# Gates, u, v and the output projection of an encoder layer by Strassen's form over two token halves

## The chip, the core and the metric

The kernel runs on one core of a Trainium2 chip. The core has TensorE (PE, matrix products into PSUM), VectorE (DVE), ScalarE (ACT), GpSimd (POOL) and SyncE (SP); each works through its own instructions in order and waits on semaphores. DMA transfers are started from the queues of SP, ACT and POOL. The metric is device time in microseconds, as the median of several runs.

## The reference

One layer of a hybrid encoder, 1024 tokens by 1024 features, fp32. What is computed, cut to what matters here:

```python
mod = silu(c) @ w_ada + b_ada                    # six vectors of 1024: sh1, sc1, gt1, sh2, sc2, gt2
h = rmsnorm(x, norm1_g) * (1 + sc1) + sh1
u, v, q, k, va, gate_a, gate_b = split(h @ w_in) # widths 512, 512, 512, 128, 128, 1024, 1024
# branch A: gelu(u) * (W_s mixed over chunks of 128 tokens of rmsnorm(gelu(v)) + b)
a_out = gmlp_branch(u, v, ...) @ w_a
# branch B: attention over |t - s| <= 128, 8 heads of 64, 2 key heads, ALiBi, a sink logit
b_out = window_attention_branch(q, k, va, ...) @ w_b
merged = sigmoid(gate_a) * a_out + sigmoid(gate_b) * b_out
x = x + gt1 * (merged @ w_o)
h2 = rmsnorm(x, norm2_g) * (1 + sc2) + sh2
f_gate, f_up = split(h2 @ w_ffn_in)              # 2816 each
x = x + gt2 * ((silu(f_gate) * f_up) @ w_ffn_out)
```

## The kernel before

**Three products for one.** fp32 precision comes from splitting both operands of a product into a rounded high part and a low part. `mm3` (line 154) issues three matmuls for each tile: high by high, high by low, low by high. A weight block of 128x1024 is made ready by `unit` (line 146): a load on SP's queue into a tile `raw`, a cast on ACT into `wh`, and a subtraction on DVE (or POOL) into `wl`. The pool `wpool` holds three of each. The same is done to activations by `split` (line 310). Nearly all matmuls are 128x128 weights by 512 columns.

**Halves.** The 1024 tokens are worked in two halves of 512 by `half(0)` and `half(1)` (line 513). Each half goes through these steps, all in one function:

- q and k: eight steps over the 1024 features. In half 0 each step also makes its slice of h and takes the dot products of the first modulation vectors (`ada_dot`, line 197; a 128x1024 multiply and sum on DVE).
- v (`v_product`, line 648), among the norms of q and k and their transposes on PE.
- attention in eight steps (the loop at line 789: `scores`, `exps`, `normalise`, `transposed`, `values`). Between these PE is kept full by `fill`, which pops parts of the products for u and for the first four gates (`u_filler`, `gate_filler`). Weight lows there are made on POOL (`prepare`).
- mixing of the gMLP branch over chunks, and its transposes.
- a loop over eight output blocks d of 128 features (line 868): two gates of 24 matmuls, two branch projections of 12, a multiply of each by its gate, their sum, and its split into `mH`, `mL`. `ada_next` loads further modulation weights and takes their dot products on DVE.
- a loop over d for w_o (line 919): 24 matmuls, the residual sum x1, its square for the next norm, a store of x1 to DRAM (`x1d`) on POOL's queue, and the modulation of h for the other half or of h2 for the FFN.

**FFN.** Behind both halves `open_ffn` closes the pools of attention and opens the FFN's. The FFN's two products over 1024 tokens are already in Strassen's form: the matrices are cut in 2x2 blocks (token halves by halves of the features), and seven block products of sums of blocks take the place of eight. Its order is written out by hand under `tc.manual_schedule()` (line 1281).

**What sets the order.** Loads on SP's queue keep the program's order (`load`, line 126), first in, first out. Instructions of PE, DVE, ACT and POOL keep it where `in_order[0]` is true (the recorder `Engine.call`, line 75, through which every operation goes; so most rows of the profile say L75). Elsewhere a scheduler orders them by readiness, and the written program decides among equals. Tiles come from pools with a fixed number of buffers: `mid` has 8 of 128x2048, `hpool` 4, `t2` 4 of 128x512. PSUM has two groups of four banks, `mm` and `at`. A load whose tile is still being read waits, and with it what stands behind it on SP's queue.

Of the kernel before, what the change touches and what calls it, by code (L numbers as in the profile page):

```python
# [38 lines left out]
def kernel(  # L39
# [48 lines left out]
    hpool = ctx.enter_context(pool("hpool", 4))  # L88
    mid = ctx.enter_context(pool("mid", 8))
# [3 lines left out]
    psum = ctx.enter_context(pool("psum", 4, space=PSUM))  # L93

# [23 lines left out]
    def hid():  # L118
        return hpool.tile([P, 2048], F32R, tag="h", name=nm("h")).rearrange(
            "p (a b) -> p a b", a=4  # L120
        )
# [9 lines left out]

    def after(ins, prev):
# [8 lines left out]
    def raw_unit(src):  # L141
        r = wpool.tile([P, UNIT], F32, tag="raw", name=nm("raw"))
        load(r, src)
        return r
# [80 lines left out]

    apool_ctx = ExitStack()
# [3 lines left out]
    silu_c = apool.tile([P, D], F32, tag="silu_c", name="silu_c")  # L230
# [236 lines left out]
    EARLY = 6  # L467
    firsts, raw2 = {}, []
    ffn_ctx = ExitStack()
    fps = []  # L470

    def open_ffn():

        apool_ctx.close()
        fp = ffn_ctx.enter_context(pool("ffn"))
        fps.append(fp)
        for part in range(2):
            t = fp.tile([P, 2048], F32R, tag=f"b22{'hl'[part]}", name=nm("first"))
            firsts[part] = t
# [15 lines left out]
    sums = []  # L495
    ada_queue = (
# [12 lines left out]

    def x_rows(hf, k):  # L510
        return xT[k * P : (k + 1) * P, hf * HALF : (hf + 1) * HALF]

    def half(hf):
# [62 lines left out]
        for k in range(KT):  # L576
# [23 lines left out]
            elif k == 0:  # L600
                wq, wk = early.pop(0), early.pop(0)
# [24 lines left out]
        if hf == 0:  # L626
            attention_constants()
        else:
            col_rstd(sums[0], NT, rcol[2])
# [5 lines left out]
        wvs = [unit(w_v[0], V)]  # L635
# [12 lines left out]
        def v_product(k):  # L648
            wv = wvs[k // 2]
            o = (k % 2) * 512  # L650
            for t in range(NT):
                cols = slice(t * P, (t + 1) * P)
                mm3(vps[t], (hH[k // 4][:, k % 4, cols], hL[k // 4][:, k % 4, cols]),
                     (wv[0][:, o : o + 512], wv[1][:, o : o + 512]), k == 0, k == KT - 1)

        srcs = [w_u[k] for k in range(4)] + [w_gb[0], w_ga[0], w_gb[1], w_ga[1], w_s]
        srcs += [w_ab[0], w_ab[1]]
        units = []
        ups = []
        gates0 = []  # L660

        due = [0]

        def prepare(eng=G):
            if srcs:
                units.append(unit(srcs.pop(0), eng))
# [855 lines left out]
```

## Time and profile before

| | |
|---|---|
| median of 3 runs | 1257.25 us (1256.49 to 1257.72) |
| profiled execution, span | 1255.1 us |
| PE, PE weight load | 1234.1 us, 1025.1 us |
| DVE, ACT, POOL | 861.5 us, 543.5 us, 132.7 us |
| DMA | 214.25 MB, mean 171 GB/s |
| chain that ended last | PE 86%, DVE 6%, ACT 3%, DMA 3% |

The profiled execution is one run under the hardware profiler; its span is the time from its first to its last recorded event, 2.15 us below the median of the timed runs. A group row names the line, the engine, the operation, output and inputs by the program's names, the shape and the count; then the total busy time and the mean of one in ns; then the idle time of the engine in front of them and what ended it. A busy engine can be a stretched one: matmuls overlap, so that the mean of a PE row (390 ns) is longer than the step from one matmul to the next.

### The profile page before, as it was taken

Reading aid. Unit: us, or ns where it says so; the run is one execution under the profiler, and the core shown is the slowest. Engines: PE = TensorE matmul, PEld = TensorE weight load, DVE = VectorE, ACT = ScalarE, POOL = GpSimd, SP = SyncE. Lnnn points to the kernel's source line nnn. Section 1 sums busy time; section 2 is a strip of 40 time slices with the busy share of each in tenths; the row PEclk is TensorE's granted clock in tenths of the full one; section 3 lists DMA queues with packets and bytes.
Section 4 is the critical chain, followed back from the end, with each engine's and each line's share of the span. In section 5 each row is a group of like instructions: output and inputs, shape, how many; then the busy total and the mean of one; then the engine's idle time right before and its main releaser. Section 6 shows DMA issues by size and latency. Waiting matters only on the chain.

```text
span 1255.1 us, 15405 instructions
## 1 busy us (share of the span) xinstructions
PE 1234.1 (98%) x5714; PEld 1025.1 (82%) x5714; DVE 861.5 (69%) x1404; ACT 543.5 (43%) x867; POOL 132.7 (11%) x148
## 2 busy tenths in 40 slices
PE   5999999999999999999999999999999999999998
PEld 4888888888888888888888888888888887888887
DVE  8998875557468786666698766666666666455646
ACT  5467853334257772334454333333333334433342
POOL 0123310000032330000100000001010000010001
PEclk9999999999999999999999999999999999999999
DMA  9422145546522126665712454464554449896652
GB/s 362 169 84 67 52 143 184 177 159 211 197 70 67 51 89 196 201 194 209 250 36 102 147 189 151 154 213 182 205 189 180 168 168 357 280 328 187 196 161 101
DMA packets 67773, 214.25 MB, mean 171 GB/s; under 512 B 7793, under 2 KB 7793, under 8 KB 62450
## 3 DMA queue, kind: packets, MB, share of 16 engines
q1 hardware_dynamic: 56450, 155.59, 37.5%
q0 software_dynamic: 11248, 57.68, 12.7%
q8 instruction: 45, 0.74, 0.2%
q14 instruction: 30, 0.25, 0.1%
HBM read 170.24 MB, written 42.99 MB: 170 GB/s over the span
## 4 chain that ended last, share of the span: by engine, by line
PE 86%; DVE 6%; ACT 3%; DMA 3%; issue 1%; SPq 0%; POOL 0%; ACTq 0%; DVEq 0%
PE mm L75 47%; PE at L75 39%; DVE mid L75 2%; DVE wl L75 2%; ACT wh L75 1%; DMA mid<-in_w_ada_dram 1%; DMA hs<-in_xT_dram 1%; ACT lb L75 1%; DVE xs L75 0%; DMA mid<-in_xT_dram 0%; ACT mid L75 0%; DVE ws L75 0%; DMA raw<-in_w_o_dram 0%; DVE hid L75 0%; DMA raw<-in_w_q_dram 0%
## 5 line engine op out<-in xcount | busy, mean ns | idle before, releaser
L75 DVE TENSOR_TENSOR wl<-raw,wh 128x1024 fp32r<-128x1024 f32 x147 | 180.7, 1231 | 122.9 <-ACT wh L75 121.5
L75 ACT CAST wh<-raw 128x1024 fp32r<-128x1024 f32 x161 | 168.9, 1053 | 218.7 <-PE mm L75 126.7
L75 PE MATMUL mm<-mid,wh 128*128 128x512 f32 x736 | 227.8, 390 | 0.8 <-DVE mid L75 0.6
L75 PE MATMUL mm<-h,wh 128*128 128x512 f32 x608 | 187.9, 390 | 0.0
L75 PEld LDWEIGHTS mm<-mid,wh 128*128 128x128 f32 x736 | 137.7, 188 | 30.3 <-DVE mid L75 1.0
L75 PE MATMUL mm<-mid,wl 128*128 128x512 f32 x368 | 143.2, 389 | 0.0
L75 PEld LDWEIGHTS mm<-h,wh 128*128 128x128 f32 x608 | 113.7, 188 | 23.4
L75 PE MATMUL mm<-wh,h 128*128 128x512 f32 x384 | 129.7, 399 | 2.4 <-ACT h L75 2.3
L75 PE MATMUL mm<-h,wl 128*128 128x512 f32 x304 | 118.3, 389 | 0.0
L75 DVE TENSOR_TENSOR wl<-ws,wh 128x1024 fp32r<-128x1024 f32 (+1 forms) x55 | 62.0, 1128 | 43.6 <-ACT wh L75 43.6
L75 PEld LDWEIGHTS mm<-wh,h 128*128 128x128 f32 x384 | 71.7, 189 | 17.3 <-ACT h L75 3.2
L75 PEld LDWEIGHTS mm<-mid,wl 128*128 128x128 f32 x368 | 69.1, 188 | 14.4
L75 ACT CAST wh<-ws 128x1024 fp32r<-128x1024 f32 (+1 forms) x55 | 53.6, 974 | 58.6 <-DVE ws L75 42.1
L75 PE MATMUL mm<-wl,h 128*128 128x512 f32 x192 | 75.9, 395 | 0.0
L75 PE MATMUL at<-h,wh 128*128 128x512 f32 x240 | 74.1, 390 | 0.0
L75 PEld LDWEIGHTS mm<-h,wl 128*128 128x128 f32 x304 | 57.1, 188 | 12.0
L75 DVE SCALAR_TENSOR_TENSOR raw<-raw,silu_c 128x1024 f32<-128x1024 f32 x32 | 39.1, 1222 | 34.4 <-DMA raw<-in_w_ada_dram 33.5
L75 DVE TENSOR_TENSOR ol<-raw,oh 128x1024 fp32r<-128x1024 f32 x30 | 36.7, 1224 | 31.6 <-ACT oh L75 29.8
L75 ACT ACTIVATE xs<-xs 128x512 f32<-128x512 f32 x21 | 13.3, 633 | 96.4 <-DVE xs L75 96.4
L75 PE MATMUL at<-wl,wh 128*128 128x512 f32 x136 | 53.0, 390 | 0.7 <-DVE wl L75 0.7
L75 PE MATMUL at<-wh 128*128 128x512 f32 x136 | 53.0, 390 | 0.4 <-DVE mid L75 0.4
L75 PE MATMUL at<-wh,wl 128*128 128x512 f32 x136 | 52.9, 389 | 0.0
(244 smaller groups left out, 2459.8 us busy)
## 6 DMA issues: line engine op xcount, KB each, us to landing
raw<-in_w_ada_dram SPq DMA_DIRECT2D x32, 512.0 KB, 3.5
raw<-in_w_gate_dram SPq DMA_DIRECT2D x28, 512.0 KB, 4.1
tA<-hid POOLq DMA_DIRECT2D x11, 1024.0 KB, 5.0
tB<-hid POOLq DMA_DIRECT2D x11, 1024.0 KB, 4.9
wo<-in_w_out_dram POOLq DMA_DIRECT2D x22, 512.0 KB, 6.3
wS<-wo POOLq DMA_DIRECT2D x11, 1024.0 KB, 5.2
raw<-wS SPq DMA_DIRECT2D x44, 256.0 KB, 3.7
raw<-tB SPq DMA_DIRECT2D x44, 256.0 KB, 4.6
```

Of the source, the lines that this page charges most:

```text
L75: ins = f(*args, **kw)
```

## The change

Strassen's form, which the FFN had, is now used for three more products: both gates together with u and v (they share h), and w_o. The 2x2 blocks of the activations are feature halves by token halves, so that products need sums of h over both token halves; work that stood in each half moves into one stage behind both attentions.

- **Pools.** `hpool` is gone (`hid` takes from `mid`, now 12 buffers); a pool `j` of 6 buffers opens behind the attentions. Ten DRAM arrays hold intermediate results. `astore` stores from ACT's queue (56 transfers).
- **Half 0.** The squares of the other half's x are summed on POOL during q and k (`x_square`), and its modulation runs in attention (`x_mod`), both with their own loads. PE's work among the norms is `bridge_product` (the two feature halves of h times w_u, kept apart); fillers are the products with w_ga. Partial results go to DRAM (`uvd`, `gd`). `u_sums` makes the sums of w_u and w_v blocks on POOL, 128x1024 each, and stores them.
- **Half 1.** `block_sums` reloads the two halves' modulated x (four loads of 1 MB) and makes the blocks T3, T4, n2, t1 during q and k. The bridge takes the sums of w_u and w_v; the fillers take the sums of w_ga and w_gb (`gate_raw_sum`, added on POOL).
- **u and v** are completed by three products of 48 matmuls with DVE sums between (`uv_product`, `uv_out`), and `v_chain` normalises v.
- **Loop over d.** `gate_prep` loads both gate weights and the stored partial gates and makes five sums of 128x512 on POOL; `gate_step` runs three groups of 12 matmuls, each followed by a sum from PSUM on DVE and a tanh. `project` makes four projections of 12 matmuls (two branches, two halves). `merge` adds them and, for d below 6, stores the merged tile on SP's queue. `ada_two` loads 1 MB of modulation weights and takes two dots; there are two of them in each turn up to d = 5.
- **w_o** is laid out in four 512x512 blocks and computed by seven products of 48 matmuls. Block sums of the weights are made on POOL (`wsum`, eight of 128x1024), those of the merged tiles on DVE (`fsum`, `block`). x1, its squares, its stores (on ACT's queue) and the modulation of h2 follow each product.

Matmuls of 512 columns go from 4988 to 4796; those of other sizes are as many as before.

```diff
-    hpool = ctx.enter_context(pool("hpool", 4))
-    mid = ctx.enter_context(pool("mid", 8))
+    mid = ctx.enter_context(pool("mid", 12))
...
+    def ada_two():
+        if not ada_queue:
+            return
+        i = ada_queue[0][0] - GT1
+        r = jt(F32, 2)
+        load(r, w_ada2[i : i + 2].rearrange("a p b -> p a b"))
+        for a in range(2):
+            col, gain = ada_queue.pop(0)
+            ada_dot(r[:, a, :], col)
+            ada_end(col, gain)
...
+    def block_sums(k, hH, hL):
+        if k == 0:
+            for i, (name, src) in enumerate((("a0", x0d), ("a1", x0d), ("b0", x1sd), ("b1", x1sd))):
+                blk[name] = midt(F32, 4)
+                load(blk[name], src[i % 2 * 4 : i % 2 * 4 + 4].rearrange("a p b -> p a b"))
...
+        if k == 1:
+            V.tensor_tensor(flat(b1), flat(b1), flat(b0), op=ALU.subtract)
...
-        def v_product(k):
-            wv = wvs[k // 2]
+        def bridge_product(k):
+            wv = bridge[k // 2]
...
+        def gate_raw_sum(d):
+            r = wpool.tile([P, UNIT], F32, tag="raw", name=nm("raw"))
+            load(r, w_gb[d])
+            x = stream("hs")
+            load(x, w_ga[d][:, :Q])
+            G.tensor_tensor(r[:, :Q], r[:, :Q], x, op=ALU.add)
+            return r
...
+                return [lambda: G.tensor_tensor(a[:, 1], a[:, 0], a[:, 1], op=ALU.add),
+                        lambda: G.tensor_tensor(a[:, 0], a[:, 0], b[:, 0], op=ALU.add),
...
+    jpools.append(ffn_ctx.enter_context(pool("j", 6, reuse_waits="tile")))
...
+    def uv_product(us, t, first):
+        for k in range(4):
+            w, o = us[k // 2], (k % 2) * 512
+            for i in range(NT):
+                cols = slice(i * P, (i + 1) * P)
+                for j, (p, q) in enumerate(((0, 0), (0, 1), (1, 0))):
+                    T.matmul(ubank[i], t[p][:, k, cols], w[q][:, o : o + 512],
+                             start=first and k + j == 0, stop=k == 3 and j == 2,
+                             skip_group_check=True)
...
+    def gate_prep(d):
+        ga, gb = raw_unit(w_ga[d]), raw_unit(w_gb[d])
+        g = gates[d] = jt(F32, 4)
+        load(flat(g), gd[d])
+        G.tensor_tensor(gb[:, Q:], gb[:, :Q], gb[:, Q:], op=ALU.add)
+        G.tensor_tensor(gb[:, :Q], ga[:, :Q], gb[:, Q:], op=ALU.add)
+        G.tensor_tensor(ga[:, Q:], ga[:, Q:], gb[:, :Q], op=ALU.add)
+        for i in (1, 3):
+            G.tensor_tensor(g[:, i, :], g[:, i, :], g[:, 2, :], op=ALU.add)
+        u = unit(None, V, gb)
+        h, l = tmp(F32R), tmp(F32R)
+        split(ga[:, Q:], h, l)
+        gunits[d] = u, (h, l)
+        A.activation(g[:, 0, :], g[:, 0, :], AF.Tanh, scale=0.5)
...
+    for d in range(KT):
+        wab = wabs[d]
+        if d:
+            gate_step(d, 2)
+        gate_step(d + 1, 0)
+        if d:
+            project(d, wab, 1, 0)
+            project(d, wab, 1, 1)
+        else:
+            project(d, wab, 0, 0)
+        gate_step(d + 1, 1)
+        if d + 2 < KT:
+            gate_prep(d + 2)
+        if d:
+            project(d, wab, 0, 0)
+        if d < KT - 1:
+            wabs[d + 1] = unit(w_ab[d + 1])
+        project(d, wab, 0, 1)
...
+        for hf in range(2):
+            merge(d, hf)
+        if d < 6:
+            ada_two()
+            ada_two()
...
+    def wsum(out, a, b):
+        for j in range(2):
+            js = slice(j * UNIT, (j + 1) * UNIT)
+            G.tensor_tensor(flat(out)[:, js], flat(a)[:, js], flat(b)[:, js], op=ALU.add)
...
+    oprod(wu, M11, sA, True)
...
+    block("M21", mf[1, 0])
+    wu = ounits(1)
+    h2m.append(xload(0, 0))
+    wsum(wq4[0], wq4[0], wq4[2])
+    wq4[4] = jt(F32, 4)
+    wsum(wq4[4], wq4[0], wq4[3])
...
+    fsum(t3f, m22, m12, ALU.subtract)
+    fsum(m12, m11, m12, ALU.subtract)
...
+    oprod(wu, blk["M21"], sB, True)
+    block("n2", m11)
+    wu = ounits(4)
...
+    oprod(wu, blk["n2"], sA, False)
+    wsum(wq4[1], wq4[1], wq4[4])
+    wsum(wq4[2], wq4[2], wq4[3])
+    block("T3", t3f)
...
+    oprod(wu, blk["T3"], sA, False)
+    block("T4", m21)
...
+    oprod(wu, blk["T4"], sA, False)
...
+    oprod(wu, blk["t1"], sB, True, range(2))
+    col_rstd(ss, NT, rcol[2])
...
+    oprod(wu, blk["M22"], sB, False)
```

More of the change, by code (lines that the diff above doesn't have):

```diff
@@ L467 @@
     EARLY = 6
+    Q = HALF
     firsts, raw2 = {}, []
[L469 to L479, printed above, removed]
     def first_unit(i):
@@ L495 @@
     sums = []
+    spare = []
+    outs = []
     ada_queue = (
@@ new lines, in ssq, with keep_x1 @@
+    def ssq(x, first, ss, eng=G):
+        if first:
+            A.activation(ss, x, AF.Square)
+        else:
+            q = tmp()
+            A.activation(q, x, AF.Square)
+            eng.tensor_tensor(ss, ss, q, op=ALU.add)
+    def keep_x1(q, hf, d, x):
+        r = (4 * q + d) * P
+        astore(x1d[r : r + P, hf * HALF : (hf + 1) * HALF], x)
+    sA = [at_bank() for _ in range(4)]
+    oprod(wu, M11, sA, True)
+    for i in (2, 3):
+        load_wo(i)
+    load_m(0, 1)
+    block("M21", mf[1, 0])
```

695 lines of the change are left out of this document (492 added, 203 removed).

## The prediction

> **What bounds the kernel now.** I read the page first, for the shares of the engines. The columns are busy time, share of the span, and instructions.
>
> ```profile
> span 1255.1 us, 15405 instructions
> PE 1234.1 (98%) x5714; PEld 1025.1 (82%) x5714; DVE 861.5 (69%) x1404; ACT 543.5 (43%) x867; POOL 132.7 (11%) x148
> PE   5999999999999999999999999999999999999998
> DVE  8998875557468786666698766666666666455646
> POOL 0123310000032330000100000001010000010001
> PEclk9999999999999999999999999999999999999999
> GB/s 362 169 84 67 52 143 184 177 159 211 197 70 67 51 89 196 201 194 209 250 36 102 147 189 151 154 213 182 205 189 180 168 168 357 280 328 187 196 161 101
> ```
>
> PE is busy in every slice but the first, and the clock is never lowered. A busy share of PE can hide half-speed streaming, so the chain that ended last comes next (start, length, what), and then what PE waited for (total, times, longest).
>
> ```profile
> 168.83 109.05 PE mm L75 x481
> 464.33 111.60 PE mm L75 x491
> ```
>
> ```profile
> PE at L75 <- DVE ss L75: 8.4, 1, 8.4
> PE at L75 <- DMA crow<-in_c_dram: 2.4, 1, 2.4
> PE mm L75 <- ACT h L75: 2.3, 2, 1.8
> ```
>
> In the two middle stretches 481 matmuls follow each other in 109.05 us: 0.2267 us each. The waits are nearly all of the start, whose loads and first norm the change leaves alone. The view by stretches of time shows the stages: first half (33 to 328 us), second half (328 to 610), FFN.
>
> ```profile
> 0.00:33.00 33.00, 19.60 (x75) 14.84 (x76) 29.04 (x54) 17.74 (x28) 2.25 (x9) 1.00 0.94 365
> 33.00:80.00 47.00, 46.48 (x259) 39.98 (x258) 42.31 (x95) 22.91 (x50) 12.87 (x11) 1.00 0.35 122
> ...
> 120.00:169.00 49.00, 48.73 (x262) 41.47 (x261) 40.95 (x99) 40.44 (x89) 18.48 (x12) 1.00 0.18 56
> 169.00:285.00 116.00, 116.00 (x521) 96.08 (x520) 68.34 (x102) 38.48 (x51) 2.35 (x2) 1.00 0.54 177
> ...
> 610.00:1250.00 640.00, 638.40 (x2819) 527.08 (x2818) 420.46 (x540) 240.52 (x304) 41.22 (x74) 1.00 0.55 186
> sum 1250.00, PE 1233.13 PEld 1024.61 DVE 860.30 ACT 543.48 POOL 132.72; mean PE 102.76 PEld 85.38 DVE 71.69 ACT 45.29 POOL 11.06
> ```
>
> The columns are window, length, busy time and count of PE, PEld, DVE, ACT, POOL, then granted clock, DMA share, GB/s. PE bounds every stage behind 33 us. DVE is close behind it in the first stage (42.31 of 47) and in attention (40.95 of 49), and has room in the gates (68.34 of 116). So fewer matmuls shorten the run as long as nothing late is put before them, and there is little else to gain: behind 33 us PE is idle 1217 − (1233.13 − 19.60) = 3.5 us.
>
> **The change part by part.** *Matmuls removed.* Gates, u and v were 1152 matmuls of 512 columns in both halves (768 + 192 + 192); seven products for eight leave 1008. For w_o 384 become 336. That is 192 fewer, at 0.2267 us: −43.5 us, all in stages where PE streams without a gap. Ideal span: 1255.1 − 43.5 = 1211.6 us. Everything below is a wait that the new sums and reloads may put before PE. The durations for it:
>
> ```profile
> L75 DVE TENSOR_TENSOR wl<-raw,wh 128x1024 fp32r<-128x1024 f32 x147 | 180.7, 1231 | 122.9 <-ACT wh L75 121.5 <-DMA raw<-tA 1.0
> L75 ACT CAST wh<-raw 128x1024 fp32r<-128x1024 f32 x161 | 168.9, 1053 | 218.7 <-PE mm L75 126.7 <-PE at L75 38.0 <-issue 26.7
> L75 DVE SCALAR_TENSOR_TENSOR raw<-raw,silu_c 128x1024 f32<-128x1024 f32 x32 | 39.1, 1222 | 34.4 <-DMA raw<-in_w_ada_dram 33.5 <-DVE t L75 0.8
> L75 POOL TENSOR_TENSOR wl<-raw,wh 128x1024 fp32r<-128x1024 f32 x14 | 33.7, 2405 | 0.7
> L75 DVE TENSOR_TENSOR wo<-wo 128x512 f32<-128x512 f32 x44 | 30.1, 684 | 0.2
> L75 DVE SCALAR_TENSOR_TENSOR t<-t,mm 128x512 f32<-128x512 f32 x32 | 21.9, 684 | 10.5 <-PE mm L75 10.5
> L75 POOL TENSOR_TENSOR mid<-xs,mid 64x512 fp32r<-64x512 f32 x16 | 21.2, 1325 | 132.8 <-ACT mid L75 85.6 <-PE at L75 47.2
> L130 POOL DMA_DIRECT2D x1d<-t x8 | 4.5, 564 | 40.4 <-DVE t L75 40.4
> ```
>
> ```profile
> raw<-in_w_ada_dram SPq DMA_DIRECT2D x32, 512.0 KB, 3.5
> tA<-hid POOLq DMA_DIRECT2D x11, 1024.0 KB, 5.0
> mid<-in_w_ada_dram SPq DMA_DIRECT2D x8, 1024.0 KB, 9.0
> out_dram<-mid SPq DMA_DIRECT2D x4, 256.0 KB, 2.0
> ```
>
> No 128x512 add on POOL is in the trace; I take the 64x512 one, 1.33 us, since the elements of a row are as many. Upper bounds below let every conflict land on PE; the lower ones are 0, because none of these pieces removes a wait.
>
> POOL and DVE hinder each other. The first fence is POOL's timeline, the second DVE's (start, length):
>
> ```profile
> 102.53 2.41 POOL L75 TENSOR_TENSOR wl<-raw,wh 128x1024 fp32r<-128x1024 f32 x1
> 118.66 2.40 POOL L75 TENSOR_TENSOR wl<-raw,wh 128x1024 fp32r<-128x1024 f32 x1
> ```
>
> ```profile
> 104.26 0.69 DVE L75 TENSOR_TENSOR es<-rows,nmx 128x4 f32<-128x4 f32 x1
> 106.03 0.16 DVE L75 TENSOR_TENSOR den<-den,es 128x4 f32<-128x4 f32 x1 [1.07 <-ACT es L75]
> 120.87 0.22 DVE L75 TENSOR_TENSOR es<-rows,nmx 128x4 f32<-128x4 f32 x1
> ```
>
> A sum of 128x4 takes 0.16 us, but 0.69 when it starts under POOL's subtraction, and it ends with that: 104.26 + 0.69 = 104.95 against 102.53 + 2.41 = 104.94; again 121.09 against 121.06. [...]
>
> *First q/k stage.* Added: seven POOL adds of the other half's squares, 7 × 1.33 = 9.3 us, eight loads on SP's queue, eight ACT squares and eight stores on POOL's queue. DVE would be at 42.3 + 9.3 = 51.6 in a window of 47: 0 to 4.6. POOL runs partly beside DVE's reads of PSUM: 2 taken.
>
> *First attention.* The v evictions, gelu and the v norm leave DVE (4 + 4 + 4 of 0.68, three squares, about 10 us); the modulation of the other half's x arrives (8 × 2 of 0.7, 11 us), and POOL gets eight weight sums (8 × 2.4 = 19 us), on which DVE's small sums stand as in the fence above. 0 to 6; 1 taken, as POOL's lows of before already cost DVE such waits without a wait of PE.
>
> *Second q/k stage.* Four 1 MB reloads on SP's queue stand ahead of wq's loads, and DVE takes a 128x2048 sum (twice 1.23) before the low of the first k weights. The last two reloads start when attention's last gate parts free their tiles: at the peak slice of 362 GB/s 5.8 us, by the tA row up to 10, + 2.5 + 1.2 = 9.5 to 13.7 us; PE has 49 matmuls of 512 columns and three of 256 left by then, 11.5 us. 0 to 6; 2 taken for this and for four more such sums.
>
> *u and v products.* Three products of 48 matmuls (10.9 us) go through the same four banks, and DVE reads the banks between them (4 × 0.68); the v norm of the first half stands in DVE's order ahead of the second read. About 0.5 + 2 + 0.5: 3 taken, 0 to 6. The sums of stored parts (two POOL adds of 2048, 4.8 us each by the 1024 row) lie beside the first product.
>
> *Front of the gates (d = 0).* The stored attention output comes back on POOL's queue, 2 MB, 10 us by the tA row, under the gate steps and the mixing. 0 to 6; 2 taken.
>
> *Loop over d.* PE has 36 gate and 48 projection matmuls: 84 × 0.2267 = 19.0 us. DVE has three gate sums and four products from PSUM (7 × 0.68), two lows of 1.23 and one of 0.68, two merges of 0.68, four modulation dots of 1.22: 14.1 us. POOL has five adds, 6.6 us. Neither fills 19 us, so only their order can stall PE. That is a chain from turn to turn: merged tile stored (2.0), then on SP's first-in-first-out queue 2 MB of modulation weights and 1 MB of gate weights behind it (3.1 MB at 362 GB/s: 8.7), three POOL adds (4.0), cast (1.05), low of the weights (1.23) and of their sum (0.68), w_ab's low (1.23), two products and two merges (2.7) = 21.6 us a turn. Over five turns it falls 5 × 2.6 = 13 us behind; the 36 gate matmuls of the next d (8.2 us) cover part: 5 taken, 0 to 15. The upper end has each pair of modulation loads land as in the crowded row of 9.0.
>
> *w_o by seven products.* 336 matmuls, 76.2 us. From the last merge to the third product PE has two products, 2 × 48 × 0.2267 = 21.8 us. In that time DVE has two half-tile blocks (8 × 0.68), four weight lows (4.9), three sums of 2048 (7.4) and four gated adds (2.7): 20.5 us, nearly all with two SBUF inputs; POOL has the first four of eight sums of w_o's blocks (4 × 2.4 = 9.6). Wholly exclusive that is 30.1 us, 8.3 more than PE has; beside each other nothing. 0 to 15, the upper end with the other four sums in the same way; 6 taken, nearer to the exclusive end, because little of DVE's work there reads PSUM.
>
> *Norm and last product.* The seventh product waits for x1's second product and its modulations stand on DVE ahead of the lows that FFN needs; before, w_o of the second half hid that under eight blocks of 24 matmuls. 0 to 8; 3 taken.
>
> *At nothing.* 56 stores move to ACT's queue: ACT is busy 43% and each store follows an ACT operation on its data; if issuing held ACT as the 564 ns of a POOL store hold POOL, 32 us would spread over 570. The FFN keeps its instructions; its streaming window (638.4 of 640) is untouched.
>
> Sum of the waits: 2 + 1 + 2 + 3 + 2 + 5 + 6 + 3 = 24. Span 1255.1 − 43.5 + 24 = 1235.6 us. The median shown, 1257.25, stands 2.15 above the profiled span; with that, 1237.8, said as 1238. All lower ends: 1213.8. All upper ends (4.6 + 6 + 6 + 6 + 6 + 15 + 15 + 8 = 66.6): 1280.
>
> **The rivals.** *POOL and DVE exclude each other (slower).* For it: the fences above, and 6.6 us of POOL adds in each of eight turns, 19.2 us in w_o and 9.3 in the first stage, 81 us in stages that PE must keep full. Against it: DVE's seven PSUM operations in a turn need not wait. It decides when more than 43.5 / 81 = 54% of that time reaches PE; at 75% the waits are 61 and the time is 1257.25 − 43.5 + 61 = 1275.
>
> *Everything hidden.* For it: DVE had 48 us of room in 116 in the gates and the FFN runs DVE at 66% with PE full; a lag of DVE is taken up as long as PE has gate matmuls to issue. Against it: the boundaries of products have no other work for PE. Waits of 0 to 10: 1214 to 1224, said as 1218.
>
> *The transfers set the loop.* 5.2 MB a turn (2.1 of modulation weights, 1.05 gate weights, 0.52 w_ab, 1.05 stored gates, 0.52 merged) in 19.0 us is 275 GB/s; slices reached 357 and 280. For it: those slices stand where loads were queued, not steady. Against it: SP can run ahead while tiles are free. At 201 GB/s, one of the busier slices of the middle, a turn takes 26 us: 6 turns × 7 = 42 more, 1257.25 − 43.5 + 42 = 1256, no change.
>
> **How the numbers follow.** Forecast (waits 11 to 40, 1225 to 1254) 0.52; hidden 0.20; transfers, no change, 0.06; POOL and DVE 0.22. I take 0.2% of 1257, 2.5 us, as what a measurement of this kernel can tell from no change. Faster 0.72, same 0.05, slower 0.23 (one hundredth of the transfers falls there). The range 1214 to 1270 leaves out about one part in ten at each end; the forecast's own is 1225 to 1254.
>
> **What would show it.** PE matmuls 192 fewer, at 0.227 us still. In the loop over d, PE busy against 19 us a turn: a turn of 21 confirms the chain, and the releaser of PE tells which rival is right: the gate weights' low with POOL adds ending at the same moment (exclusion), or loads landing late (transfers). In w_o, a wait before the third product. Wrong would make me: PE full in those stages (hidden), or waits mainly in the two q/k stages, where I take only 4 us.

## The result, and the profile after

The changed kernel takes 1311.75 us (median of 4 runs, 1307.18 to 1313.22); the kernel before, beside it, 1256.87. The ratio is 1.0433, with a 95% interval of 1.0415 to 1.0452: 4.3% slower. The prediction said 1238, with a range of 1214 to 1270.

The page of the changed kernel, the lines that answer to those shown of before:

```profile
span 1310.3 us, 15346 instructions
PE 1230.9 (94%) x5522; PEld 1003.2 (77%) x5522; DVE 961.1 (73%) x1445; ACT 568.5 (43%) x928; POOL 281.6 (21%) x229
PE   6879998999969998988999999999999999999998
DVE  8999868977587776789899766766665765555646
POOL 1583320433362242263010001000001000010001
PEclk9998999999989999998999999999999999999999
```

The 192 matmuls are gone (5714 to 5522), but PE's busy time fell by only 3.2 us, because some matmuls became slower (0.43 us a step for 0.227, below): the clock line has eights, which before had none. POOL works 149 us more, DVE 100 us more; an operation that is held up counts as busy (a copy of 0.23 us stands with 2.27 in the fence of DVE below). By stages (window, length, then busy time and count of PE, PEld, DVE, ACT, POOL, then granted clock with 1.00 as full speed, DMA share, GB/s): first q and k, first attention, second q and k with its attention, u and v products, gate loop, output projection, FFN.

```profile
22.00:63.00 41.00, 36.09 (x192) 31.15 (x192) 40.48 (x63) 17.95 (x34) 21.59 (x21) 1.00 0.86 327
63.00:190.00 127.00, 111.20 (x548) 90.19 (x547) 108.89 (x236) 83.60 (x193) 57.57 (x35) 0.94 0.57 206
190.00:348.00 158.00, 150.89 (x755) 125.29 (x755) 115.81 (x247) 96.98 (x202) 49.17 (x34) 0.98 0.60 215
348.00:395.00 47.00, 34.80 (x146) 27.89 (x145) 41.33 (x46) 27.57 (x51) 26.83 (x16) 0.87 0.46 169
395.00:575.00 180.00, 170.30 (x740) 137.50 (x739) 129.53 (x192) 47.62 (x66) 53.85 (x33) 0.97 0.63 240
575.00:655.00 80.00, 68.51 (x282) 53.59 (x282) 75.77 (x77) 35.98 (x54) 26.04 (x10) 0.94 0.28 101
655.00:1300.00 645.00, 643.46 (x2815) 526.73 (x2814) 427.61 (x550) 245.77 (x312) 44.79 (x75) 1.00 0.54 186
```

PE is idle for 4.9, 15.8, 7.1, 12.2, 9.7, 11.5 and 1.5 us in them, 62.7 us together, where before it was idle 3.5 behind 33 us. Five of the seven also show a clock below 1. What PE waited for (total, times, longest) is mostly DVE:

```profile
PE at L75 <- DVE wl L75: 14.2, 8, 3.1
PE mm L75 <- DVE mid L75: 9.4, 5, 6.5
PE at L75 <- DVE qhl L75: 8.9, 3, 6.0
...
PE mm L75 <- DVE j L75: 4.9, 1, 4.9
```

And DVE stood behind POOL. The first fence is DVE's timeline in the changed kernel (start, length of the group, count at the end), the second POOL's:

```profile
81.78 2.27 DVE L75 COPY kd<-kd 128x128 f32<-128x128 f32 x1
83.96 2.59 DVE L75 SCALAR_TENSOR_TENSOR kd<-kraw,krs,gqk 128x64 f32<-128x64 f32 x2
...
92.01 0.23 DVE L75 COPY kd<-kd 128x128 f32<-128x128 f32 x1
...
96.58 4.51 DVE L75 TENSOR_TENSOR qhl<-mid,qhl 128x256 fp32r<-128x256 f32 x2 [0.47 <-ACT qhl L75]
...
574.62 11.30 DVE L75 TENSOR_TENSOR mid<-mid,mid 128x512 fp32r<-128x512 f32 x4
...
600.36 2.48 DVE L75 TENSOR_TENSOR mid<-mid,mid 128x512 fp32r<-128x512 f32 x4
```

```profile
81.59 2.37 POOL L75 TENSOR_TENSOR mid<-mid 128x1024 f32<-128x1024 f32 x1
...
95.64 5.17 POOL L75 TENSOR_TENSOR mid<-mid,mid 128x1024 f32<-128x1024 f32 x2
...
568.16 11.61 POOL L75 TENSOR_TENSOR j<-j,mid 128x1024 f32<-128x1024 f32 x4 [31.72 <-DMA mid<-in_w_o_dram]
```

A copy that takes 0.23 us takes 2.27 while POOL makes a weight sum. Four lows of the output projection take 11.3 us beside POOL's sums of w_o, and 2.48 us without them.

Last, the clock. Two windows of PE (the column behind the busy time is the granted clock), and PE's timeline behind the wait of 6.0 us at 92 to 99 us:

```profile
96.20:106.40 10.20, 5.88 (x19) 0.50 0.77 280
106.40:116.60 10.20, 10.20 (x58) 1.00 0.66 234
```

```profile
101.76 0.76 PE L75 MATMUL mm<-wh,mid 128*128 128x512 f32 x1
102.31 0.63 PE L75 MATMUL mm<-wl,mid 128*128 128x512 f32 x1
102.74 1.05 PE L75 MATMUL mm<-wh,mid 128*128 128x512 f32 x2
103.59 0.63 PE L75 MATMUL mm<-wl,mid 128*128 128x512 f32 x1
```

From 102.31 to 102.74 one matmul takes 0.43 us, where it takes 0.227 at full clock. The mean clock of the run is 0.979; with 0.50 as the lowered clock, as in the first window, it was lowered for 4.2% of the run, 55 us. Adding up over the matmuls in these stretches what each step is longer than 0.2265 gives some 20 us.

### The profile page after: what moved, and what is told of

Same layout as the page of the kernel before. It is cut to its first block, busy times and chain, and to the rows that moved or that the text cites. A ratio compares the mean times of both kernels' runs of the same rounds, so it can differ in the third digit from the quotient of the medians.

```text
span 1310.3 us, 15346 instructions
## 1 busy us (share of the span) xinstructions
PE 1230.9 (94%) x5522; PEld 1003.2 (77%) x5522; DVE 961.1 (73%) x1445; ACT 568.5 (43%) x928; POOL 281.6 (21%) x229
## 4 chain that ended last, share of the span: by engine, by line
PE 64%; DVE 16%; DMA 10%; ACT 4%; issue 4%; POOL 1%; SPq 0%; ACTq 0%; DVEq 0%; POOLq 0%
PE at L75 40%; PE mm L75 24%; DVE mid L75 7%; DMA raw<-in_w_gb_dram 3%; DVE wl L75 3%; DVE j L75 2%; DMA raw<-in_w_q_dram 1%; ACT wh L75 1%; DMA mid<-in_xT_dram 1%; DVE kd L75 1%; POOL raw L75 1%; DMA mid<-in_w_ada_dram 1%; DMA md<-j 1%; DMA mid<-x0d 1%; ACT lb L75 1%
## 5 line engine op out<-in xcount | busy, mean ns | idle before, releaser
L75 PE MATMUL at<-mid,wh 128*128 128x512 f32 (+1 forms) x728 | 228.7, 396 | 6.1 <-ACT mid L75 2.9
L75 PEld LDWEIGHTS at<-mid,wh 128*128 128x128 f32 x728 | 138.6, 192 | 38.2 <-ACT mid L75 3.3
L75 PE MATMUL at<-mid,wl 128*128 128x512 f32 (+1 forms) x364 | 144.1, 396 | 8.9 <-DVE wl L75 8.9
L75 PE MATMUL at<-j,wh 128*128 128x512 f32 (+1 forms) x464 | 143.6, 391 | 0.0
L75 PE MATMUL mm<-wh,mid 128*128 128x512 f32 x320 | 110.8, 414 | 11.6 <-DVE mid L75 6.5
L75 PEld LDWEIGHTS at<-j,wh 128*128 128x128 f32 x464 | 86.5, 188 | 20.2 <-DVE mid L75 0.2
L75 PE MATMUL at<-j,wl 128*128 128x512 f32 (+1 forms) x232 | 90.7, 391 | 0.0
L75 PEld LDWEIGHTS at<-mid,wl 128*128 128x128 f32 x364 | 69.8, 192 | 25.5 <-DVE wl L75 11.0
L75 PEld LDWEIGHTS mm<-wh,mid 128*128 128x128 f32 x320 | 63.0, 200 | 25.7 <-ACT mid L75 13.3
L75 PE MATMUL mm<-wl,mid 128*128 128x512 f32 x160 | 66.4, 415 | 0.4 <-DVE wl L75 0.4
L75 DVE TENSOR_TENSOR ol<-raw,oh 128x1024 fp32r<-128x1024 f32 x30 | 36.7, 1224 | 32.4 <-ACT oh L75 30.6
```

The source lines that it names most:

```text
L75: ins = f(*args, **kw)
```

## The experiments

**Whose time is it: POOL's sums on DVE.** One theory was that POOL and DVE exclude each other, the rivals that DVE is simply full, or that the chains wait whoever adds. Four runs moved added sums from POOL to DVE by changing the engine of the instruction.

```diff
 # e1: u_sums, all four sums of each call
-                return [lambda: G.tensor_tensor(a[:, 1], a[:, 0], a[:, 1], op=ALU.add),
+                return [lambda: V.tensor_tensor(a[:, 1], a[:, 0], a[:, 1], op=ALU.add),
 # e2: gate_prep, its five sums, and the two sums of 2048 of the u and v stage
-        G.tensor_tensor(gb[:, Q:], gb[:, :Q], gb[:, Q:], op=ALU.add)
+        V.tensor_tensor(gb[:, Q:], gb[:, :Q], gb[:, Q:], op=ALU.add)
 # e3: wsum, and the squares of the output projection
-            G.tensor_tensor(flat(out)[:, js], flat(a)[:, js], flat(b)[:, js], op=ALU.add)
+            V.tensor_tensor(flat(out)[:, js], flat(a)[:, js], flat(b)[:, js], op=ALU.add)
-    def ssq(x, first, ss, eng=G):
+    def ssq(x, first, ss, eng=V):
 # e4: all of these, x_square and gate_raw_sum
-            G.tensor_tensor(ssn, ssn, q, op=ALU.add)
+            V.tensor_tensor(ssn, ssn, q, op=ALU.add)
```

> The eight weight sums of w_u and w_v (128x1024 each, 82 to 104 us of the changed kernel's timeline) run on DVE in place of POOL; everything else is as changed. Theory A, exclusion of POOL and DVE: in that stretch a DVE copy of 128x128 took 2.27 us in place of 0.23, so the four waits of PE there (2.4, 1.5, 6.3, 2.1 us) shrink although DVE gets 8 x 1.23 = 9.8 us more, and with them the half-clock time around 96 to 106 us. 1311.75 less 8 to 15: 1297 to 1304 us. Theory B, DVE is simply full there: 9.8 us more of it stand before PE, 1316 to 1322 us. Theory C, the waits come from the chain of norms and transposes, whoever adds: within 3 us of 1311.75.

> The five adds of 128x512 in each turn of the gate loop's preparation, and the two sums of 128x2048 ahead of the second u and v product, run on DVE in place of POOL. Theory A, exclusion: the waits between 348 and 575 us (gaps of 6.5, 4.9, 2.3, 2.9, 2.9 us and about 9 us lost at half clock) shrink by half or more, although DVE gets 8 x 5 x 0.68 + 2 x 2.3 = 32 us more over 227 us: 1290 to 1300 us. Theory B, DVE full: a turn's DVE work goes from 14.1 to 17.5 us against 19.0 of PE, so waits of the same size: 1308 to 1316 us. Theory C, the loads on the first-in-first-out queue set the loop: within 3 us in the loop, but the gaps at 361 and 386 us go: 1298 to 1303 us.

> In the output projection the eight sums of weight blocks (128x1024) and the sums of squares run on DVE in place of POOL. Theory A, exclusion: in the changed kernel four lows of 128x512 took 11.3 us (2.74 alone) beside POOL's sums, so the waits of PE between 585 and 617 us (3.9, 2.9, 0.8, 1.5 us and about 4 us lost at half clock) shrink, although DVE gets 8 x 1.23 + 7 x 0.69 = 15 us more: 1300 to 1307 us. Theory B, DVE full: DVE was busy 90 of 100 us from 575 to 675, 15 us more stand before PE: 1312 to 1325 us.

> All added POOL sums run on DVE: those of the three kernels before this one, the squares of the other half's x in the first q and k stage, and the sums of w_ga and w_gb in the second attention. Theory A, exclusion: most of the waits of PE (about 65 us of gaps and 21 us lost at half clock more than in the kernel before) go: 1240 to 1275 us. Theory B, DVE full: 1300 us or more. If the three single moves add up, this one is 1311.75 less their sum, within 6 us.

| moved to DVE | median us | against 1311.75 |
|---|---|---|
| weight sums of u and v | 1303.79 (1299.35 to 1307.37) | −8.0 |
| sums of gates, and of stored u and v parts | 1290.38 (1286.49 to 1291.16) | −21.4 |
| sums of w_o and of squares | 1308.75 (1308.26 to 1309.71) | −3.0 |
| all | 1278.51 (1274.18 to 1279.87) | −33.2 |

Every median fell, although DVE got more to do. The third fell by less than the four runs of the changed kernel spread, so its gain is not clear of noise. The three single moves add up to −32.4, with all at −33.2, so that the two further moves (`x_square`, `gate_raw_sum`) gave next to nothing. The first lies in the range of the exclusion theory, the second at its edge. The third stayed short of its range: DVE was nearly full there (75.77 of 80 us in the changed kernel), and in e4 PE still waits 4.0 us for a low at 572 us that stands behind sums which nothing needs yet. All together is above the 1240 to 1275 expected and 1.65% above the kernel before (ratio 1.0165, 1.0146 to 1.0185). So the order of the exclusion theory holds, and it is not all. In the gate loop a move also makes the sums themselves shorter (0.68 us on DVE, 1.3 on POOL).

**The exclusion by itself, in the kernel before.** Eight sums of no use, 128x1024, at the two places of the first attention where the change makes its weight sums; nobody waits for them. Once on POOL (e11), once on DVE (e12).

```diff
+        def extra():
+            o = midt(F32, 2)
+            for a in range(4):
+                G.tensor_tensor(o[:, a % 2, :], hH[0].rearrange("p a b -> p (a b)")[:, :UNIT].bitcast(F32),
+                                hL[0].rearrange("p a b -> p (a b)")[:, :UNIT].bitcast(F32), op=ALU.add)
+        if hf == 0:
+            extra()
         v_product(2)
...
+            if t == 0 and hf == 0:
+                extra()
```

> The kernel before with eight sums of 128x1024 of no use added on POOL (inputs and output in SBUF), at the two places in the first attention where the changed kernel makes its weight sums; no loads, no stores, nothing waits for the sums. Theory A, exclusion: POOL's 8 x 2.4 us hold up DVE's small operations as in the changed kernel, and PE waits for DVE: 8 to 16 us longer, 1265 to 1273 us. Theory B, work on an engine off the path costs nothing: within 2 us of 1257.

> The same eight sums added on DVE in place of POOL in the kernel before: 8 x 1.23 = 9.8 us more DVE work ahead of PE's transposes, no exclusion. Theory A (exclusion is the larger evil): 3 to 8 us longer than before, less than the run with POOL. Theory B (DVE full): more than the run with POOL, 8 to 12 us longer than before.

Measured: on POOL 1274.98 us (1274.57 to 1275.25), ratio 1.0146 (1.0131 to 1.0161), 18.3 us more than the kernel before beside it (1256.64). On DVE 1268.80 (1267.88 to 1270.34), ratio 1.0100 (1.0083 to 1.0117), 12.2 more. Both are larger than the first theory had it; its order, POOL worse than DVE, holds. The kernel with POOL's sums shows why they cost so much. DVE's timeline, then POOL's:

```profile
80.00 2.26 DVE L75 COPY kd<-kd 128x128 f32<-128x128 f32 x1
82.19 4.67 DVE L75 SCALAR_TENSOR_TENSOR kd<-kraw,krs,gqk 128x64 f32<-128x64 f32 x2
...
93.79 0.23 DVE L75 COPY kd<-kd 128x128 f32<-128x128 f32 x1
```

```profile
75.14 18.54 POOL L75 TENSOR_TENSOR mid<-h,h 128x1024 f32<-128x1024 f32 x8
```

The two engines take turns here: one POOL sum, one small DVE operation, one POOL sum. Each DVE operation, the copy of 0.23 us as well, takes 2.26 to 2.34 us, about as long as one sum (18.54 / 8 = 2.32), until POOL has no more at 93.68 us. The waits that this gives PE come with 17.07 us of half clock. What is paid is not POOL's share of a shared resource but 2.3 us for each step of a chain.

**What if the sums cost nothing.** All added POOL sums left out.

```diff
-            G.tensor_tensor(ssn, ssn, q, op=ALU.add)
+            pass
-            G.tensor_tensor(r[:, :Q], r[:, :Q], x, op=ALU.add)
-                return [lambda: G.tensor_tensor(a[:, 1], a[:, 0], a[:, 1], op=ALU.add),
...
+                return [lambda: store(usd[j], flat(a)), lambda: store(utd[j], flat(b))]
-    G.tensor_tensor(flat(c2), flat(c2), flat(up1), op=ALU.add)
-    G.tensor_tensor(flat(c1), flat(c1), flat(up1), op=ALU.add)
-        G.tensor_tensor(gb[:, Q:], gb[:, :Q], gb[:, Q:], op=ALU.add)
...
-    wsum(wq4[0], wq4[0], wq4[2])
-    wq4[4] = jt(F32, 4)
-    wsum(wq4[4], wq4[0], wq4[3])
+    wq4[4] = wq4[3]
...
```

> The changed kernel with all its added POOL sums left out (the weight sums for u and v, gates and output projection, the sums of stored parts and of squares); loads, stores, products and DVE's block sums stay, so that the output is not the reference's. It shows what the change would take if the sums cost no engine anything. Theory A, nearly all of the lost time comes from these sums, by POOL and DVE excluding each other and by DVE's load once they are moved there: 1215 to 1235 us. Theory B, the new structure (reloads, stage boundaries, block sums on DVE, half clock behind its waits) has a large part of its own: 1245 to 1270 us; with the sums all on DVE it was 1278.5, with them on POOL 1311.75.

Measured: 1247.75 us (1246.55 to 1248.53), ratio 0.9929 (0.9914 to 0.9944). This splits the loss. The added sums cost 1311.75 − 1247.75 = 64.0 us on POOL and 1278.51 − 1247.75 = 30.8 on DVE. Without them 1247.75 − (1257.25 − 43.5) = 34.0 us of loss stay: Theory B has a part. Even with free sums the change would gain 0.7%. The stages of this kernel, first attention and gate loop:

```profile
100.00:172.00 72.00, 67.14 (x334) 53.92 (x332) 58.18 (x147) 54.56 (x125) 21.84 (x13) 1.00 0.53 177
...
363.00:535.00 172.00, 172.00 (x782) 141.94 (x781) 126.92 (x202) 50.92 (x69) 0.00 (x0) 1.00 0.64 243
```

In the gate loop of this kernel PE is never idle, with the same loads and stores at 243 GB/s. So the transfers do not limit it, and the chain through SP's queue no longer does once POOL's adds are out of it.

**Relieving DVE beside the move.** e7 is e4 with evictions on ACT, an earlier norm, the output projection's sums behind the lows that PE waits for, and 32 bytes of padding (below). e8 also moves the weight sums of u and v to the end of the first attention.

```diff
 # e7
-                (V.tensor_copy if t % 2 else A.copy)(u[:, t, :], vps[t])
+                A.copy(u[:, t, :], vps[t])
-            (V.tensor_copy if t % 2 else A.copy)(qraw[:, t, :], qps[t])
+            A.copy(qraw[:, t, :], qps[t])
...
         kr = kv_norms(banks, nkv)
+        if hf == 0:
+            col_rstd(next_x["ss"], NT, rcol[1])
...
-    wsum(wq4[1], wq4[1], wq4[4])
-    wsum(wq4[2], wq4[2], wq4[3])
     block("T3", t3f)
+    wu = ounits(0)
...
     wu = ounits(3)
+    wsum(wq4[1], wq4[1], wq4[4])
+    wsum(wq4[2], wq4[2], wq4[3])
 # e8
+        if hf == 0:
+            us = u_sums(0)
         run_jobs(99)
...
-(("a0", x0d), ("a1", x0d), ("b0", x1sd), ("b1", x1sd))
+(("b0", x1sd), ("b1", x1sd), ("a0", x0d), ("a1", x0d))
```

> All added sums on DVE as in the run where all moved, and DVE relieved where it was full: evictions of q, k and of the partial u and v all on ACT (8 copies of 512 less on DVE in each half), the other half's norm taken ahead of q's on POOL, in the output projection the weight sums and one block sum behind the lows that the next product waits for, the last squares back on POOL, and the 32 bytes of padding. Theory: what is left there behind the exclusion is DVE's own order and load: the waits at 77 to 99 us (3.3 and 4.8) and at 572 us (4.0) go, 1278.5 less 10 to 20: 1258 to 1268 us. If the waits that are left come from the chains of loads and reloads instead: 1272 us or more (the padding alone counts up to 6).

> As the run before it in this call, and the eight weight sums of w_u and w_v moved from the front of the first attention to its end, where DVE has room, with the reloads for the second q and k stage in the order of use. Theory: DVE's load at the front is what is left of the stall there: 5 to 10 us below the run before it in this call, 1250 to 1260 us, level with the kernel before. Rival: their loads and stores then crowd the second q and k stage's reloads: equal or slower than the run before it.

Measured: e7 1279.95 us (1277.46 to 1281.18), no better than e4; e8 1288.39 (1285.17 to 1290.52), worse. In e7 the wait at 572 us is gone, but one of 3.1 us behind ACT's evictions and a longer one ahead of the FFN came in its place. In e8 the rival held. This is its longest wait:

```profile
PE mm L75 <- ACT wh L75: 20.0, 3, 19.3
```

The cast of the second half's first weights waits, at 188 to 207 us, for a load that stands on SP's queue behind the reloads of x, and these wait for tiles until the sums in them are stored (8.3 us for the store). No version that computes the whole layer beat the kernel before.

**What the first attention loses without the sums.** e9, and DVE's part of the modulation of the other half's x left out too, its lows replaced by copies on ACT.

```diff
-                    V.scalar_tensor_tensor(out=xk, in0=xk, scalar=mod[:, SC1 + k : SC1 + k + 1],
-                                           in1=next_x["rb"], op0=ALU.mult, op1=ALU.mult)
...
-                V.scalar_tensor_tensor(out=lo, in0=next_x[k], scalar=mod[:, SH1 + k : SH1 + k + 1],
-                                       in1=hi.bitcast(F32), op0=ALU.add, op1=ALU.subtract)
+                A.copy(lo, next_x[k])
```

> The kernel without the added sums, and in the first attention also without DVE's part of the modulation of the other half's x (eight multiplies left out, eight lows replaced by copies on ACT, so that the output is not the reference's): 12 us less on DVE there, 5 us more on ACT. Theory A, DVE's load in the first attention makes its waits (8.4 us of gaps, 1.7 at half clock): they go, 1247.75 less 5 to 9: 1239 to 1243 us. Theory B, the order of norms, transposes and evictions makes them: within 2 us of 1247.75.

Measured: 1251.29 us (1251.23 to 1251.58), 3.5 more than e9, in the range of neither theory. Taking 12 us from DVE did not shorten these waits, against Theory A, but ACT got 5 us more to do at the same time. The waits for the evictions of attention's output grew, e9 first, e13 second:

```profile
PE at L75 <- DVE xs L75: 4.8, 6, 1.2
```

```profile
PE at L75 <- DVE xs L75: 6.9, 6, 1.6
```

The DVE sum `xs` follows an ACT copy, and ACT is the engine that got more work. That ACT's order is the cause was not tried by itself.

**The FFN.** Its instructions are as before, but it is slower. The same stretch of 324 us up to the same point of the FFN, of before and of after:

```profile
715.10:1039.10 324.00, 323.84 (x1427) 1.00 0.51 179
```

```profile
770.20:1094.20 324.00, 324.00 (x1411) 1.00 0.50 178
```

That is 0.2270 and 0.2296 us a matmul, with the clock at 1.00. Only the matmuls that read tiles of the new pool `j` are slower: the mean of their steps is 0.233 us, that of those reading `mid` 0.227. The last 2600 matmuls take 597.3 us in place of 592.3. Three runs looked for the cause: the change adds a constant of 32 bytes that puts every large tile 32 bytes off a multiple of 64, and it opens the pool with an option.

```diff
 # e5, the changed kernel
+    const.tile([P, 8], F32, tag="pad", name="pad")
 # e6, the kernel before, with the same line
 # e14, the changed kernel
-    jpools.append(ffn_ctx.enter_context(pool("j", 6, reuse_waits="tile")))
+    jpools.append(ffn_ctx.enter_context(pool("j", 6)))
```

> The changed kernel with a constant of 32 bytes per partition added in front of the tile pools, nothing else. The change added one constant of 32 bytes there, so that every large tile begins 32 bytes off a multiple of 64; in the kernel before they begin on multiples of 64. In the FFN, whose matmuls did not change, matmuls that read tiles of the new pool step at 0.233 us in place of 0.227, and its last 2600 matmuls take 597.3 us in place of 592.3. Theory A, the offset causes it: those steps go back to 0.227 and the run to 1303 to 1308 us. Theory B, it is the place of the pool or traffic beside it: steps stay at 0.233, 1309 to 1313 us.

> The kernel before with a constant of 32 bytes added in front of its pools, so that its large tiles begin 32 bytes off a multiple of 64. Theory A (offset): the FFN's matmuls step at 0.23 or more and the run takes 3 to 12 us longer than before, 1260 to 1269 us. Theory B (place or traffic): no change within 2 us of 1256.8.

> The changed kernel with the new pool's buffers handed on in the ordinary way (without the option that waits by tile). Theory A, that option costs the FFN's matmuls on those tiles their 6 ns: steps go back to 0.227 us and 1303 to 1307 us. Theory B, it does not: steps stay at 0.233 us, 1309 to 1315 us.

Measured: e5 1306.67 us (1302.5 to 1312.49); the steps stay at 0.233 and the last 2600 matmuls at 597.6 us in the profiled execution, the one of 1312.49. Its runs overlap those of the changed kernel, so the lower median is not clear of noise. e6 1257.38 (1255.97 to 1258.43), ratio 1.0001 (0.9991 to 1.0010), steps unchanged. e14 1309.79 (1308.91 to 1312.0), 597.9 us. Neither the offset nor the option is the cause. These 5 us stay open.

**The clock.** Does it follow PE's waits? The first try (e10) put matmuls of no use into three waits of the changed kernel, the second (e15) and the third (e16) into one.

```diff
 # e10
+    def keep_warm(n):
+        bank = at_bank()
+        for _ in range(n):
+            T.matmul(bank, zeros, identr.unsqueeze(1).to_broadcast([P, 4, P]), start=True, stop=True)
...
+            if hf == 0 and t == 1:
+                keep_warm(20)
             q_transpose(q0, qs[t // 2][:, (t % 2) * 8 : (t % 2) * 8 + 8, :])
...
+    keep_warm(24)
     uv_product(ws, T1J, False)
...
+    keep_warm(16)
     gate_step(0, 1)
 # e15: 26 of them ahead of uv_product(ws, T1J, False); e16: ahead of uv_product(ws, B22, False),
 # both in program order
+    in_order[0] = True
+    bank = at_bank()
+    for _ in range(26):
+        T.matmul(bank, zeros, identr.unsqueeze(1).to_broadcast([P, 4, P]), start=True, stop=True)
     uv_product(ws, B22, False)
+    in_order[0] = False
```

> The changed kernel with 20, 24 and 16 matmuls of no use (512 columns, into a bank that is overwritten) put on PE into three of its waits: ahead of the second q transpose of the first half (wait of 6.0 us), ahead of the second u and v product (6.5 us) and ahead of the second gate step (4.9 us). They take 4.6, 5.5 and 3.6 us, less than each wait. Theory A, the granted clock is halved because PE waits: in the changed kernel it was half from 96.2 to 106.4, 365.8 to 372.6 and 389.7 to 396.5 us, right behind these waits, where matmuls of 512 columns stepped at 0.43 us; these three stretches vanish, and the run gets 6 to 11 us shorter, 1301 to 1306 us. Theory B, the clock goes by something else: the stretches stay and the time is 1311 to 1316 us.

> The changed kernel with 26 matmuls of no use (5.9 us, into a bank of their own) directly ahead of the second u and v product, where PE waits 6.5 us and where the clock is half for 6.8 us from 365.8 us on. Theory A, the clock is halved by PE's idle time: the half-clock stretch there is gone, the next 12 to 16 matmuls step at 0.23 in place of 0.43, and the run is 2 to 4 us shorter, 1308 to 1310 us. Theory B, it is not: the stretch stays, 1311 to 1314 us.

> The changed kernel with 26 matmuls of no use (5.9 us, into a bank of their own) directly ahead of the third u and v product, where PE waits 6.5 us for DVE and where the clock is half for 6.8 us from 365.8 us on. Theory A, the clock is halved by PE's idle time: that half-clock stretch is gone and the first matmuls of the product step at 0.23 us in place of 0.43; 2 to 4 us shorter, 1308 to 1310 us. Theory B, it goes by something else: the stretch stays, 1311 to 1314 us.

e10 took 1319.52 us (1316.84 to 1321.49) and tells nothing: behind its first 20 matmuls the transposes waited 5.6 us in one piece for DVE (`kbuf`), its last 16 waited 3.0 us themselves, and the wait of 6.6 us in the u and v stage stayed, because it is ahead of the third product. e15 (1307.98, 1304.24 to 1312.01) repeated the second mistake. e16 hit the place. PE's timeline:

```profile
361.67 6.08 PE L75 MATMUL at<-identr,zeros 128*128 128x512 f32 x26
368.51 0.47 PE L75 MATMUL mm<-wh,mid 128*128 128x512 f32 x1 [0.75 <-DVE mid L75]
368.81 0.39 PE L75 MATMUL mm<-wl,mid 128*128 128x512 f32 x1
369.04 0.40 PE L75 MATMUL mm<-wh,mid 128*128 128x512 f32 x1
372.30 0.50 PE L75 MATMUL mm<-wh,mid 128*128 128x512 f32 x1 [2.86 <-DVE mid L75]
...
374.25 0.63 PE L75 MATMUL mm<-wl,mid 128*128 128x512 f32 x1
374.68 1.05 PE L75 MATMUL mm<-wh,mid 128*128 128x512 f32 x2
```

Kept busy, PE starts the product at full clock (0.23 us from 368.81 to 369.04), where the changed kernel ran at half. It then meets a second wait of 2.86 us that had been hidden in the first, and the half clock comes behind that, from 373.7 to 377.1 us. So Theory A holds as far as one place can show it. The time did not fall (1313.3, 1311.48 to 1319.2); at this place the second wait brought the half clock back. The kernels e11 and e12 say the same from the other side: the kernel before has no half clock behind its start, and with waits put in by the useless sums it has 17.1 and 6.8 us of it, among them and directly behind.

## Why the prediction was wrong

**The saving** held as the prediction worked it out: 192 matmuls of 0.227 us are gone. What failed is the sum of the waits, 24 us taken, 66.6 with all upper ends, 1310.3 − 1211.6 = 98.7 measured.

| term | taken (upper end) | idle of PE after | lost at half clock |
|---|---|---|---|
| first q/k stage | 2 (4.6) | 4.9 | 0 |
| first attention | 1 (6) | 15.8 | 5 |
| second q/k stage, with attention | 2 (6) | 7.1 | 2 |
| u and v products | 3 (6) | 12.2 | 4 |
| front and loop over d | 2 + 5 (21) | 9.7 | 5 |
| output projection, norm, last product | 6 + 3 (23) | 11.5 | 4 |
| FFN | 0 | 1.5 (1.6 before) | 0; 5 by slower steps |

The third column adds to 62.7, of which 3.5 stood there before; the fourth adds to 20, and the FFN's slower steps to 5. The rest of the 98.7, some 14 us, no run put to a cause.

**The step that failed first** is "POOL and DVE hinder each other", as the forecast then used it. The prediction had the row (0.69 us for 0.16) and the right reading of it. DVE's reads of PSUM, which it let run beside POOL, did keep their time: in the kernel before all 44 of `pL<-at,pH` take 0.67 to 0.69 us, also the two that lie under POOL's low of 102.53 us (103.06 us, 1.28 for both). But it priced each conflict by POOL's time against the room in the stage, and for the first attention it took 1 us "as POOL's lows of before already cost DVE such waits without a wait of PE". That term measured 15.8 us of idle PE and 5 at half clock. Before, one POOL low fell in a step of 8 us with matmuls to cover it. Eight sums in a row make a chain of small DVE operations pay 2.3 us for nearly each, and it is on this chain that PE's transposes wait: 18.3 us for eight sums in e11. Room does not help a chain. The u and v products are the second term far above its upper end of 6: PE's waits of 6.5 and 4.9 us there fell to 2.5 and 1.3 with the sums on DVE (e2).

**The rival** with this mechanism named the pair of engines rightly, but its size came near by luck. It said 61 us, three quarters of 81 us of POOL's time in the loop, in w_o and in the first q/k stage. It left out the eight sums of the first attention, the stage that lost most, and the sums of stored parts. The sums cost 64.0 us (e9), while POOL worked 149 us more; 30.8 us of cost stay with the sums on DVE, so that at most half, 33.2, is owed to their place on POOL. Its time of 1275 was too low because it set every other wait to nothing, and 34 us are of that kind. Its chance of 0.22 was too low for the reason above: room in a stage was counted as cover for a chain.

**The step that was missing** is the clock. The prediction read "the clock is never lowered" from a kernel in which PE hardly waits, and carried it over to one with waits. (The row reads full clock even up to 26 us, where matmuls of 512 columns step at 0.43 us in both kernels.) The half clock costs some 20 us. In the stages of the changed kernel each wait of 2.2 us or more is followed by a stretch at half clock, which lasts 3.4 us or a multiple of it (6.8, 10.2); one more stretch, from 188.3 us on, came behind a wait of 1.1 us. In the profiles of all kernels here, behind the start, half clock began during each of 41 waits of 3.5 us or more that began at full clock, or within 3.5 us of its end; the same holds for 49 of 58 waits between 2.2 and 3.5 us, and for 20 of 138 between 1 and 2.2.

**The loop over d** was thought bound by the chain through SP's queue, 21.6 us a turn, and that is what the trace shows. POOL's first add of a turn starts at 439.69, 461.60, 483.82, 506.26 and 528.49 us: 22.2 us a turn. These are pieces of the chain that ended last in the changed kernel, over one turn (start, length, what):

```profile
431.05 8.51 DMA raw<-in_w_gb_dram
...
439.69 1.30 POOL raw L75
...
441.06 1.31 POOL raw L75
442.38 1.06 ACT wh L75
...
444.73 1.79 DVE t L75
446.52 2.30 DVE j L75 x2
...
449.56 2.29 DMA md<-j
...
452.86 8.60 DMA raw<-in_w_gb_dram
```

Gate weights land, POOL adds, ACT casts, DVE makes the lows, the merged tile is stored, and behind that store on SP's queue the next loads start. What failed is the cover: of the 13 us by which the chain falls behind, 5 were taken, since gate matmuls of the next d would hide part. The stage lost 9.7 us of idle PE and 5 at half clock. The two causes meet in this chain: POOL's adds stand in it, and they hold up the DVE operations behind them, such as the low `t`, 1.79 us here and 0.69 in e2. With the adds on DVE a turn takes 20.3 us (e2); without them PE was busy 172.00 of 172.00 us (e9), as the prediction's own terms have it, 21.6 − 4.0 = 17.6 against 19.0. Of the 21.4 us that e2 gained, no run separates the shorter chain from the lifted exclusion. The third rival, the transfers, falls: 243 GB/s in e9 and no wait.

**The output projection** was named rightly, "a wait before the third product" at a price of 6 us: PE waits 3.9 us for a low in the second product and 2.85 and 0.8 at the third. But moving its sums to DVE gave 3.0 us at most. That DVE is the full engine there on either is the likely reason; no run relieved it alone.

**The rival "everything hidden"** falls by e9: even without the sums the kernel stays 34 us above 1213.75. In its profile PE is idle 19.8 us from 22 us to the last product, where before it was 3.5, the half clock takes some 6, and the FFN's slower steps take 5; the rest was not traced.

## What to carry to other kernels

POOL's sums on SBUF were not free work beside a busy DVE: eight that nobody waited for cost 18.3 us (e11). Ask which chain of small DVE operations runs at that moment, and price it as one POOL operation for each link, 2.3 us there. Where POOL's work stands in a chain that returns every turn, count that chain's turn against PE's: what it was longer by here, 22.2 us for 19.0, hardly hid behind matmuls of the next turn (9.7 us of idle PE). A saving on an engine that streams without a gap is bought with sums and reloads on the others; first measure the kernel with these left out, since that shows about the most that placing them better can give with the rest as it is (here 0.7%). Where a change brings waits into a gapless matmul stream, add the half clock that follows them: here it came with every wait of 3.5 us or more and with most from 2.2 us on.

## What the runs showed of the hardware that was not expected

- With POOL's sums back to back, DVE and POOL take turns, one operation each (e11); where POOL paused for 0.08 us, one more small DVE operation passed in 0.27 us (changed kernel, 83.96 us). A DVE copy with a single SBUF input (128x128, 0.23 us) is held about as long as an operation with two (`kd<-kraw,krs,gqk`, 128x64, 0.28 us): 2.26 us in e11, and 4.67 for two of the latter.
- In the changed kernel the half clock came with idle times of 1.1 to 6.5 us and lasted 3.41, 6.83 or 10.24 us; in e11, with four waits in a row, 17.07.
- The same matmuls step at 0.233 us on tiles of one pool and at 0.227 on those of another, at full clock. With all tiles shifted by 32 bytes the steps stayed at 0.233 (e5), and the kernel before took 1.0001 of its time (e6). The cause is open.
